# Gate modulation beside the output projection read through other buffers, and the last tile's residual and final products in another order

## The chip, the cores and the metric

The kernel runs on one core of a Trainium2 chip. The core has five engines that run side by side, each with its own queue of instructions in a fixed order: TensorE (PE in the profile: matmuls, with PEld for loading their weights), VectorE (DVE), ScalarE (ACT), GpSimd (POOL) and SyncE (SP), which here does nothing but issue transfers. They work on an on-chip memory, SBUF, and TensorE writes its results to a second one, PSUM, in banks. An engine waits for another through semaphores.

The metric is the device time of one execution in microseconds, as the median of several runs. The profile is one execution on the chip, recorded by the hardware; its span is a little shorter than the execution's device time.

## The reference

One inference step of a two-layer diffusion backbone, for 512 latent tokens and 128 context tokens (640 in all, width 1024). Each layer has a mixer (attention) and a SwiGLU feed-forward part; both are framed by an adaptive modulation whose shift, scale and gate come from a condition vector, one for the latent and one for the context tokens.

```python
for l in range(DEPTH):                       # 2 layers
    sh1, sc1, g1, sh2, sc2, g2 = split(silu(cond) @ w_mod[l] + b_mod[l], 6)
    h = rms_norm(x, norm_mix[l]) * (1 + sc1) + sh1
    x = x + g1 * mixer(h)                    # layer 0: MLA and neighbourhood attention, layer 1: GQA
    h = rms_norm(x, norm_ffn[l]) * (1 + sc2) + sh2
    gate, up = split(h @ w_ffn_in[l], 2)
    x = x + g2 * ((silu(gate) * up) @ w_ffn_out[l])
y = rms_norm(x, norm_final)
```

The part that matters here: `g2` of layer 1 (the product of 1024 numbers `silu(cond)` with 1024 columns of `w_mod[1]`, for two conditions) is computed while the output projection inside `mixer` of layer 1 runs; and the last addition to `x` and the last `rms_norm` end the kernel.

## The kernel before

The activations lie transposed: 8 tiles `x[0]` to `x[7]` of 128 features by 640 tokens. Work on tokens goes by halves of 320 (`HALF`; half 0 is called c = 0, half 1 c = 1). Each matmul of single precision is done as three faster ones, with both operands split into a high and a low part; so each weight tile is loaded as it is ("raw"), copied to its high part by ScalarE, and the low part is the difference, taken by VectorE (`lo="v"`) or GpSimd (`lo="g"`). That is `unit` (L172 to L182).

Buffers come from pools with a fixed number of slots for each tag. A read into a slot waits until everything that used the tile before it in that slot is done. Three pools matter: `rawp` with 3 slots for raw weights, `wp` with 3 for split ones, and `fp` (`op[5]`), the pool of the feed-forward part of layer 1, which is opened before the output projection (`ffn_open`, L1057) and lies where the attention's tiles lay.

The order on each engine's queue isn't the order in which the program is written. A planner goes through the program with its own estimates of durations: whenever an engine is free, it gives it the earliest written instruction whose inputs and slot are ready at that moment. The result is a fixed order for each queue, DMA issues on SP's among them. `after(inst, fn)` forbids the planner to put what `fn` writes ahead of `inst` on the same engine; it adds no wait at run time.

**The output projection of layer 1** is `mixer_out` (L980), with tiles named `oc`. It makes 8 output tiles n from 8 attention tiles. For n = 0 and 1 all but the last of the eight steps are done for both halves before the last attention tile is there; tiles 2 to 4 are done for both halves one after the other; for tiles 5 to 7 the second half is held back, and done in pieces between the modulations of the next part. `evac(n, c, ps)` adds a finished half to `x[n]` with its gate (`residual`, L316, two VectorE instructions for the second half), squares it on ScalarE and adds the square to a running sum on VectorE (`Norm.add`, L202). When half 0 of all tiles is summed, `rstd` (L212) sums over the features with a matmul by ones (tile `ocnp`), and two activations make the scale that the modulation of the feed-forward part waits for. A pair of PSUM banks is held by a tile from its first matmul to its eviction; there are four banks for tiles 0 to 6.

After each n, `beside(n)` is called: in layer 1 it is `gates_beside` (L1870), which computes the 8 x 2 gate products. For n = 0 to 3 it issues the reads of two raw tiles `wmG` of `w_mod`; for n = 1 to 4 it multiplies those of the step before with the two condition rows `cb`, 16 products of 128 x 1024 in all (`junkG`, with the sum in an accumulator that is read by a second short instruction). At n = 4 the bias is added. In layer 0 `beside` does nothing.

**The end of the kernel** is the last pass (p = 3) of the loop over pairs of output tiles at the end of `ffn` (L1547 on), which makes tiles 6 and 7 with a scheme of seven products for 2 x 2 blocks. Its steps are S2, A11, S3, A12, A22, S1 and S4. A12 gives half 0 of tile 6, A22 half 0 of tile 7, S1 (bank `c`) gives half 1 of tile 7 (with `u3`), and S4 (bank `d`) half 1 of tile 6, as the bank plus `p6`. `final` (L1887) does the last norm: a product of each tile's half with its weight and the scale, and the write of the result, on the queue of SP or of ScalarE by turns. Half 0's scale and first four products are written right after A22, the other four after S1; half 1's eight come at the very end.

Of the kernel before, what the change touches and what calls it, by code (L numbers as in the profile page):

```python
# [11 lines left out]
F32 = mybir.dt.float32  # L12
F32R = mybir.dt.float32r
AF = mybir.ActivationFunctionType
ALU = mybir.AluOpType
# [34 lines left out]
def body(ctx, tc, xT, vecs, crow, wm0, wm0g, wm1, wA, wNV, wNA, wMK, wMV, wOA, wGQ, wGK, wGV, wOC,  # L50
# [143 lines left out]


    class Norm:
        def __init__(self, name, n):
            self.name, self.n, self.k = name, n, [0, 0]
            self.acc = tmp(name + "acc")
            self.rs = tmp(name + "rs")  # L200

        def add(self, x, i):  # L202
            c0, c1 = HALF[i]
            if self.k[i] == 0:
                S.activation(self.acc[:, c0:c1], x[:, c0:c1], AF.Square)
            else:
                sq = tp.tile([P, HT], F32, tag="u", bufs=7, name=f"{self.name}sq{self.k[i]}{i}")
                S.activation(sq, x[:, c0:c1], AF.Square)
                V.tensor_add(self.acc[:, c0:c1], self.acc[:, c0:c1], sq)
            self.k[i] += 1  # L210

        def rstd(self, i):  # L212
# [767 lines left out]
    def mixer_out(wsrc, os_, order, xin, ml, name, nxt, pre, beside=lambda n: None):  # L980

        nrm = Norm(name + "n", D)
        oh, ol = [o[0] for o in os_], [o[1] for o in os_]
        x = []
        ks = [(k, k) for k in order]
        if True:
            def wunit(n):
                get = lazy(lambda: unit(wsrc[n], 1024, f"{name}w{n}", lo="g" if n % 2 else "v"))
                return lambda w0: (get(), w0)

            def evac(n, c, ps):
                if c == 0:
                    x.append(xin(n))
                residual(x[n], x[n], ps, ml, G1, n, c)
                nrm.add(x[n], c)

            def half(ps, un, c, ks, first=True, last=True):
                two_halves([ps], [un], ks, oh, ol, c, first=first, last=last)

            held = []  # L1000
            for n in range(KT):
                un = wunit(n)
                if n < 2:
                    ps = pair(f"{name}{n}")
                    for c in range(2):
                        half(ps, un, c, ks[:-1], last=False)
                    held.append((ps, un))
                    if n == 1:
                        for i, (ps, un) in enumerate(held):
                            for c in range(2):  # L1010
                                half(ps, un, c, ks[-1:], first=False)
                                evac(i, c, ps[c])
                        held = []
                elif n < 5:
                    ps = pair(f"{name}{n}")
                    for c in range(2):
                        half(ps, un, c, ks)
                        evac(n, c, ps[c])
                else:
                    ps = pair(f"{name}{n}") if n < 7 else [bank(f"{name}{n}{c}") for c in range(2)]  # L1020
                    half(ps, un, 0, ks)
                    evac(n, 0, ps[0])
                    held.append((n, ps, un))
                beside(n)
            pre()
            for j in range(KT - 2):
                for n, ps, un in held:
                    half(ps, un, 1, ks[j:j + 1], first=j == 0, last=False)
# [44 lines left out]
    def ffn(l, x, pend, hm, nxt, side, opened):  # L1073
# [418 lines left out]
        if paired:  # L1492
# [54 lines left out]
            for p in range(4):  # L1547
                n = 2 * p
                b = {c: bank(f"fo{l}_1_{p}{c}", "my"[p % 2]) for c in "abcd"}
                o = {c: tp.tile([P, HT], F32, tag="u", bufs=7, name=f"fo{l}_1_{p}{c}") for c in ("p1", "p6", "u3", "x")}  # L1550
                for k, (c, which, to) in enumerate(PLAN):
                    j = p * len(PLAN) + k
                    weights(j + LEAD)
                    seventh(j, b[to], which, c in ("S2", "A11", "S1", "S4"))
                    ps = b[to][:, :HT]
                    if c == "S2":
                        S.activation(o["p6"], ps, AF.Copy)
                    elif c == "A11":
                        S.activation(o["p1"], ps, AF.Copy)
                        V.tensor_tensor(o["p6"], o["p6"], o["p1"], ALU.add)  # L1560
                    elif c == "S3":
                        V.tensor_tensor(o["u3"], ps, o["p1"], ALU.add)
                    elif c == "A12":
                        evac(n, 0, b["a"])
                    elif c == "A22":
                        V.tensor_tensor(o["p1"], ps, o["p1"], ALU.add)
                        evac(n + 1, 0, o["p1"])
                        if p == 3:
                            nxt(x, nrm, 0, range(4))
                    elif c == "S1":  # L1570
                        V.tensor_tensor(o["u3"], ps, o["u3"], ALU.add)
                        V.tensor_tensor(o["p6"], ps, o["p6"], ALU.add)
                        evac(n + 1, 1, o["u3"])
                        if p == 3:
                            nxt(x, nrm, 0, range(4, KT))
                    else:
                        V.tensor_tensor(o["x"], ps, o["p6"], ALU.add)
                        evac(n, 1, o["x"])
# [291 lines left out]
    def gates_beside(n):  # L1870
        if n == 0:
            for c in range(2):
                S.activation(cb[c], cb[c], AF.Silu)
        while gates:
            i, raw = gates.pop(0)
            for c in range(2):
                junk = op[1].tile([P, D], mybir.dt.bfloat16, tag="junk", bufs=1, name=f"junkG{i}{c}")
                V.scalar_tensor_tensor(junk, raw, 1.0, cb[c], ALU.mult, ALU.mult, accum_out=mods[1][:, G2 + i, c:c + 1])
        if n < 4:
            gates.extend((i, load(wm1[G2 + i], D, f"wmG{i}")) for i in (2 * n, 2 * n + 1))  # L1880
        elif n == 4:
            m = mods[1][:, G2:G2 + 8, :]
            V.tensor_tensor(m, m, bc2(bmod(1, G2, 8)), ALU.add)
# [2 lines left out]

    def final(x, nrm, c, ks):  # L1887
        c0, c1 = HALF[c]
        if 0 in ks:
            nrm.rstd(c)  # L1890
        for k in ks:
            V.scalar_tensor_tensor(x[k][:, c0:c1], x[k][:, c0:c1], vcol(V_NFIN + k), nrm.rs[:, c0:c1], ALU.mult, ALU.mult)
            (nc.sync if k % 2 else nc.scalar).dma_start(yT[:, k, c0:c1], x[k][:, c0:c1])

    x, pend = ffn(1, x, pend, box["m"], final, lambda fk: lambda *a: None, op)
    pend()
# [156 lines left out]
```

## Time and profile before

| what | us |
| --- | --- |
| median of 3 runs (1527.66 to 1532.81) | 1528.15 |
| the profiled execution's own time | 1527.25 |
| its span in the profile | 1525.5 |
| TensorE busy in the span | 1461.0 |
| VectorE busy | 1191.0 |
| ScalarE busy | 768.8 |
| GpSimd busy | 223.3 |
| output projection of layer 1, first eviction to the last sum of half 0 | 1030.70 to 1076.80 |
| gate products, first and last start | 1025.3 to 1055.9 |
| last matmul of the feed-forward part to the end of the span | 1510.96 to 1525.5 |

How to read the lines that follow: in the timelines each line has the start, the length, the engine, the line of the program, the instruction, the tile written `<-` the tiles read, sizes, a count, and in brackets how long the engine stood idle before it and what ended that. In the chain of waits, a line has start, length, engine, tile and line. `SPq` is SyncE's queue of DMA issues. Busy times of engines that nobody waits for cost nothing.

### The profile page before, as it was taken

What the parts mean: (1) busy time and instruction counts of PE and PEld (TensorE: products, weight loads), DVE (VectorE), ACT (ScalarE), POOL (GpSimd) and SP (SyncE); (2) the same over time, 40 slices, a digit from 0 to 9 for tenths busy, and PEclk for the clock granted to TensorE, in tenths of its full rate; (3) what the DMA queues carried; (4) which work ended last, traced back from release to release, by engine and by line L of the source; (5) the groups of instructions that cost most, each with busy time, mean ns of one, the idle gap of its engine ahead of it and who ended that gap; (6) DMA issues with size and microseconds to landing.
All of it is one profiled execution on the core that took longest, in us unless ns stands there. A gap on an engine that the chain in (4) does not pass through costs nothing.

```text
span 1525.5 us, 25797 instructions
## 1 busy us (share of the span) xinstructions
PE 1461.0 (96%) x9856; PEld 1404.0 (92%) x9856; DVE 1191.0 (78%) x2233; ACT 768.8 (50%) x1506; POOL 223.3 (15%) x295
## 2 busy tenths in 40 slices
PE   5999989989999999999999999998999999999996
PEld 4888878879999999999999899987999999999996
DVE  5646687885899999968998777768798889854496
ACT  5445577763755455531224566662755555542242
POOL 0225634522000000000003333211100000000000
PEclk9999999999999999999999999998999999999998
DMA  9324540005155555479762300016244445458521
GB/s 370 115 95 167 174 142 30 27 23 189 38 187 174 192 190 183 163 248 344 237 217 95 103 29 29 28 33 203 70 136 162 161 163 196 157 208 303 209 91 69
DMA packets 79579, 226.89 MB, mean 149 GB/s; under 512 B 8816, under 2 KB 14208, under 8 KB 79328
## 3 DMA queue, kind: packets, MB, share of 16 engines
q1 hardware_dynamic: 77120, 220.84, 42.3%
q10 hardware_dynamic: 1920, 3.47, 0.7%
q8 instruction: 77, 1.26, 0.3%
q0 software_dynamic: 416, 0.93, 0.2%
q14 instruction: 46, 0.38, 0.1%
HBM read 190.86 MB, written 34.36 MB: 148 GB/s over the span
## 4 chain that ended last, share of the span: by engine, by line
PE 81%; DVE 10%; ACT 4%; DMA 2%; issue 2%; POOL 0%; DVEq 0%; SPq 0%; ACTq 0%; POOLq 0%
PE fg L62 19%; PE fd L62 9%; PE fo L62 7%; PE fu L62 5%; PE gq L62 2%; PE nk L62 2%; PE nq L62 2%; PE fo_2b L62 1%; PE fo_0b L62 1%; PE fo_0a L62 1%; PE fo_2a L62 1%; PE mod L62 1%; PE go L62 1%; PE gs L62 1%; PE ms L62 1%
## 5 line engine op out<-in xcount | busy, mean ns | idle before, releaser
L1098 ACT ACTIVATE sg<-g 128x320 f32<-128x320 f32 x40 | 18.9, 472 | 132.1 <-DVE g L1098 132.1
L1626 DVE SCALAR_TENSOR_TENSOR junk<-wm,cb 128x1024 bf16<-128x1024 f32 x62 | 75.6, 1220 | 6.1 <-DMA wm<-in_wm 5.5
L62 PE MATMUL gq<-h10h,wgq 128*128 128x320 f32 x256 | 66.4, 318 | 0.4 <-DVE gb L1809 0.3
L249 POOL TENSOR_SCALAR h10h<-h10t,gs,mods 128x320 fp32r<-128x320 f32 x4 | 3.6, 888 | 429.5 <-DVE h10t L243 427.8
L1098 DVE TENSOR_TENSOR wY<-s,wY 128x1024 fp32r<-128x1024 f32 x40 | 48.7, 1218 | 1.1 <-ACT wY L1098 1.1
L1098 DVE TENSOR_TENSOR wZ<-s,wZ 128x1024 fp32r<-128x1024 f32 x40 | 48.7, 1218 | 0.0
L62 PEld LDWEIGHTS gq<-h10h,wgq 128*128 128x128 f32 x256 | 45.3, 190 | 1.8 <-PE gtp L66 1.1
L1098 ACT ACTIVATE wZ<-s 128x1024 fp32r<-128x1024 f32 x40 | 42.4, 1061 | 2.3 <-DVE s L1098 2.2
L1098 ACT ACTIVATE wY<-s 128x1024 fp32r<-128x1024 f32 x40 | 42.0, 1049 | 0.0
L1098 DVE SCALAR_TENSOR_TENSOR junk<-wm,cb 128x1024 bf16<-128x1024 f32 x34 | 41.5, 1220 | 0.6
L1810 ACT ACTIVATE gp<-gs,gb,rq 128x640 f32<-128x640 f32 (+1 forms) x40 | 31.9, 797 | 19.0 <-DVE gb L1809 14.9
L1098 DVE TENSOR_TENSOR sg<-up,sg 128x640 f32<-128x640 f32 (+1 forms) x40 | 31.4, 785 | 12.2 <-ACT sg L1098 12.2
L62 PE MATMUL gq<-h10l,wgq 128*128 128x320 f32 x128 | 39.8, 311 | 0.0
L62 PE MATMUL fg<-h11q,wX 128*128 128x320 f32 x240 | 38.7, 309 | 0.9 <-DVE wX L181 0.9
L62 PE MATMUL fd<-h11D,wY 128*128 128x320 f32 x240 | 38.8, 309 | 0.5 <-DVE wY L1098 0.5
L62 PE MATMUL fg<-h11E,wW 128*128 128x320 f32 x240 | 38.7, 310 | 0.3 <-DVE g L1098 0.3
L62 PE MATMUL fu<-h11q,wX 128*128 128x320 f32 x240 | 38.7, 309 | 0.0
L62 PE MATMUL fg<-h11N,wZ 128*128 128x320 f32 x240 | 38.6, 309 | 0.0
L62 PE MATMUL fg<-h01q,wX 128*128 128x320 f32 x240 | 38.6, 309 | 0.0
L62 PE MATMUL fg<-h01N,wZ 128*128 128x320 f32 x240 | 38.6, 309 | 0.0
L62 PE MATMUL fu<-h01q,wX 128*128 128x320 f32 x240 | 38.6, 309 | 0.0
L62 PE MATMUL fg<-h01E,wW 128*128 128x320 f32 x240 | 38.6, 309 | 0.0
(3188 smaller groups left out, 5291.2 us busy)
## 6 DMA issues: line engine op xcount, KB each, us to landing
wm<-in_wm SPq DMA_DIRECT2D x40, 512.0 KB, 3.9
mraw<-in_wm SPq DMA_DIRECT2D x24, 512.0 KB, 3.6
mraw<-in_wm SPq DMA_DIRECT2D x8, 1024.0 KB, 15.3
hr_T<-sp_T SPq DMA_DIRECT2D x24, 320.0 KB, 5.9
hr_B<-sp_B SPq DMA_DIRECT2D x18, 320.0 KB, 6.9
wm<-in_wm0g SPq DMA_DIRECT2D x8, 512.0 KB, 3.4
wmG<-in_wm SPq DMA_DIRECT2D x8, 512.0 KB, 3.5
x<-in_xT SPq DMA_DIRECT2D x8, 320.0 KB, 5.6
```

The source lines that it names most:

```text
L62: cls.last = nc.tensor.matmul(*a, **k)
L249: G.tensor_scalar(h[:, c0:c1], t, self.gsl[:, k, 0:1], self.ml[:, self.sh + k, 0:1], ALU.mult, ALU.add)
L1098: self.last = after(self.last, lambda: op(*a, **k))
L1626: def step(kind, at, line=lambda op, *a, **k: op(*a, **k)):
L1810: S.activation(dst, src, AF.Exp, bias=nb, scale=rq[:, j:j + 1], accum_out=ll[:, j:j + 1])
```

## The change

The gate reads no longer take slots of `rawp`, but the two slots of tag `wr` in the feed-forward pool. The weight units of all eight tiles are made ahead as objects, and the unit of tile n + 1 (its read and its split) is written before the gate products of step n, for n = 1 to 6. The gate products are put behind the last sum of squares that is written by then (`nrm.last`), on VectorE.

At the end, half 0's scale is written after A22 without products. After S1, half 1 of tile 6 gets `p6` added at once by a residual of its own; then tile 7 is evicted, and one final product of half 0 is put behind its sum. After S4 the bank `d` is added to tile 6 by a second residual, without the addition that made `x` of it and `p6`; that eviction is put behind the one final product, and the other seven products of half 0 behind its sum.

```diff
     class Norm:
+        last = None
...
-                V.tensor_add(self.acc[:, c0:c1], self.acc[:, c0:c1], sq)
+                self.last = V.tensor_add(self.acc[:, c0:c1], self.acc[:, c0:c1], sq)
...
+            units = [wunit(n) for n in range(KT)]
             for n in range(KT):
-                un = wunit(n)
+                un = units[n]
...
-                beside(n)
+                if beside is not None:
+                    if 0 < n < KT - 1:
+                        units[n + 1](0)
+                    beside(n, nrm.last)
...
                         evac(n + 1, 0, o["p1"])
                         if p == 3:
-                            nxt(x, nrm, 0, range(4))
+                            nrm.rstd(0)
                     elif c == "S1":
                         V.tensor_tensor(o["u3"], ps, o["u3"], ALU.add)
                         V.tensor_tensor(o["p6"], ps, o["p6"], ALU.add)
-                        evac(n + 1, 1, o["u3"])
                         if p == 3:
-                            nxt(x, nrm, 0, range(4, KT))
+                            residual(x[n], x[n], o["p6"], mods[l], G2, n, 1)
+                            evac(n + 1, 1, o["u3"])
+                            ended = after(nrm.last, lambda: nxt(x, nrm, 0, range(0, 1)))
+                        else:
+                            evac(n + 1, 1, o["u3"])
+                    elif p == 3:
+                        after(ended, lambda: evac(n, 1, b["d"]))
+                        after(nrm.last, lambda: nxt(x, nrm, 0, range(1, KT)))
                     else:
                         V.tensor_tensor(o["x"], ps, o["p6"], ALU.add)
                         evac(n, 1, o["x"])
...
-                V.scalar_tensor_tensor(junk, raw, 1.0, cb[c], ALU.mult, ALU.mult, accum_out=mods[1][:, G2 + i, c:c + 1])
+                after(done, lambda: V.scalar_tensor_tensor(junk, raw, 1.0, cb[c], ALU.mult, ALU.mult,
+                                                           accum_out=mods[1][:, G2 + i, c:c + 1]))
         if n < 4:
-            gates.extend((i, load(wm1[G2 + i], D, f"wmG{i}")) for i in (2 * n, 2 * n + 1))
+            for i in (2 * n, 2 * n + 1):
+                raw = op[5].tile([P, D], F32, tag="wr", bufs=2, name=f"wmG{i}")
+                nc.sync.dma_start(raw, wm1[G2 + i])
+                gates.append((i, raw))
...
     def final(x, nrm, c, ks):
         c0, c1 = HALF[c]
-        if 0 in ks:
+        if 0 in ks and c == 1:
             nrm.rstd(c)
         for k in ks:
-            V.scalar_tensor_tensor(x[k][:, c0:c1], x[k][:, c0:c1], vcol(V_NFIN + k), nrm.rs[:, c0:c1], ALU.mult, ALU.mult)
+            last = V.scalar_tensor_tensor(x[k][:, c0:c1], x[k][:, c0:c1], vcol(V_NFIN + k), nrm.rs[:, c0:c1], ALU.mult, ALU.mult)
             (nc.sync if k % 2 else nc.scalar).dma_start(yT[:, k, c0:c1], x[k][:, c0:c1])
+        return last
```

More of the change, by code (lines that the diff above doesn't have):

```diff
@@ L978, in two_halves, with mixer_out @@
                 proj(pss[u][c], wh[0], wh[1], hh, hl, [k], *HALF[c], first=first and j == 0, last=last and j == n - 1, w0=wl)
-    def mixer_out(wsrc, os_, order, xin, ml, name, nxt, pre, beside=lambda n: None):
+    def mixer_out(wsrc, os_, order, xin, ml, name, nxt, pre, beside=None):
         nrm = Norm(name + "n", D)
@@ L1868, in body, with gates_beside @@
     gates = []
-    def gates_beside(n):
+    def gates_beside(n, done):
         if n == 0:
```

## The prediction

> **What bounds the kernel now.** First the page's head:
>
> ```profile
> span 1525.5 us, 25797 instructions
> PE 1461.0 (96%) x9856; PEld 1404.0 (92%) x9856; DVE 1191.0 (78%) x2233; ACT 768.8 (50%) x1506; POOL 223.3 (15%) x295
> ```
>
> TensorE is busy nearly throughout, so a change pays only where TensorE waits. Next, TensorE in order of time over the layer-1 output projection (tiles oc0 to oc7), where the gate modulation runs beside it, and the windows view of several stretches (columns: length, busy time of PE, PEld, DVE, ACT, POOL, granted clock, DMA share, GB/s):
>
> ```profile
> 1031.68 0.31 PE L62 MATMUL oc1b<-oGs7h,ocw 128*128 128x320 f32 x1
> 1039.04 0.63 PE L62 MATMUL oc2a<-oGs0h,ocw 128*128 128x320 f32 x1 [7.04 <-ACT ocw L180]
> ```
> ```profile
> 1025.30:1030.70 5.40, 5.40 (x39) 5.40 (x38) 3.69 (x6) 1.06 (x1) 0.00 (x0) 1.00 0.31 93
> 1030.70:1076.80 46.10, 38.51 (x239) 37.85 (x238) 37.81 (x61) 15.74 (x23) 9.95 (x4) 0.89 0.61 203
> 350.70:385.40 34.70, 34.70 (x239) 34.70 (x238) 22.91 (x33) 13.62 (x21) 9.85 (x4) 1.00 0.45 153
> 1041.00:1047.10 6.10, 6.08 (x23) 6.09 (x24) 4.83 (x8) 1.06 (x1) 0.26 (x1) 0.52 0.80 251
> 842.40:845.00 2.60, 2.60 (x6) 1.81 (x7) 0.10 (x1) 1.33 (x4) 0.99 (x2) 0.50 0.16 61
> 1520.00:1522.00 2.00, 0.00 (x0) 0.00 (x0) 2.00 (x6) 0.00 (x0) 0.00 (x0) 0.50 0.94 330
> ```
>
> After oc1 TensorE stops for 7.0 us, and when oc2 runs, from 1041 to 1047, it has a clock of 0.52: 23 matmuls in 6.1 us, 0.27 each, where the row 350.70:385.40 has 239 in 34.7, 0.145 each. Why is weight tile ocw2 late? The transfer queue and VectorE in order of time:
>
> ```profile
> 907.33 0.33 SPq L163 DMA_DIRECT2D ocw0r<-in_wOC  x1
> 926.00 19.27 SPq L163 DMA_DIRECT2D wmG<-in_wm  x2
> 963.20 0.33 SPq L163 DMA_DIRECT2D ocw1r<-in_wOC  x1
> 981.69 46.54 SPq L163 DMA_DIRECT2D wmG<-in_wm  x2
> 1034.50 0.33 SPq L163 DMA_DIRECT2D ocw2r<-in_wOC  x1
> ```
> ```profile
> 1033.25 1.22 DVE L1878 SCALAR_TENSOR_TENSOR junkG<-wmG,cb 128x1024 bf16<-128x1024 f32 x1
> ...
> 1039.74 1.22 DVE L181 TENSOR_TENSOR ocw<-ocw2r,ocw 128x1024 fp32r<-128x1024 f32 x1
> ...
> 1047.17 0.55 DVE L320 SCALAR_TENSOR_TENSOR xr<-oc2a,mods,xr 128x320 f32<-128x320 f32 x1 [1.23 <-PE oc2a L62]
> 1048.03 2.30 DVE L1878 SCALAR_TENSOR_TENSOR junkG<-wmG,cb 128x1024 bf16<-128x1024 f32 x1 [0.30 <-DMA wmG<-in_wm]
> ...
> 1057.20 2.40 DVE L1883 TENSOR_TENSOR mods<-mods,vec 128x16 f32<-128x16 f32 x1
> ...
> 1068.55 1.49 DVE L209 TENSOR_TENSOR ocnacc<-ocnacc,ocnsq 128x320 f32<-128x320 f32 x1 [0.54 <-ACT ocnsq L208]
> ```
>
> Gate reads and weights share three raw buffers. The read of ocw2 goes out at 1034.50, when the gate product that began at 1033.25 has freed one; then come its transfer, its split, and a queue of products before the low half at 1039.74.
>
> **The mixer stage, step by step.** Removed: four gate reads ahead of ocw2 in the raw buffers. At the moments at which those buffers came free (907, 926, 945, 963, 982) the new order can read ocw0 to ocw4; ocw2 then needs only a third split buffer, left by the last query tile. TensorE can go from oc1 at 1031.8 straight into oc2. The same function in layer 0, with no gates, shows that pace: from the first eviction to the last sum of squares of the first token half it takes 34.70 us (row 350.70:385.40, TensorE busy throughout), here 46.10 (row 1030.70:1076.80). TensorE alone would gain 11.4 us.
>
> But VectorE has to keep up, and here I chose against that number. In those 46.10 us VectorE is busy for 37.81. After the change it no longer splits ocw2 there (the row of 1039.74: -1.2), but the three products that now run before the first eviction (the 3.69 of row 1025.30:1030.70) must come behind it, since each waits for the last sum of squares. So 37.8 - 1.2 + 3.7 = 40.3 us of VectorE work in a stretch that TensorE could do in 34.7. **VectorE becomes the bound of this stage.**
>
> What else costs time? A sum waits half a microsecond for its square (0.54 in the row of 1068.55); with products at hand most of these waits are filled, though not the first ones: I take 1.2 us idle, from 0. And GpSimd's four weight splits hold VectorE:
>
> ```profile
> 1046.84 2.41 POOL L181 TENSOR_TENSOR ocw<-ocw3r,ocw 128x1024 fp32r<-128x1024 f32 x1 [35.25 <-ACT ocw L180]
> 1057.16 2.42 POOL L181 TENSOR_TENSOR ocw<-ocw5r,ocw 128x1024 fp32r<-128x1024 f32 x1 [7.91 <-DVE junkG L1878]
> 1067.19 2.50 POOL L181 TENSOR_TENSOR ocw<-ocw7r,ocw 128x1024 fp32r<-128x1024 f32 x1 [7.62 <-ACT ocw L180]
> ```
>
> The product of 1048.03, the addition of 1057.20 and the sum of 1068.55 each end just after such a pass. The product is 1.08 over the 1.22 of its kind, the addition of 16 columns at most 2.3 over, the sum 1.0 if without the pass it takes a third of its time: 4.4 us of GpSimd's 9.95. The eviction of 1047.17, which reads PSUM, isn't held. In a fuller VectorE more of the 9.95 is met: I take 1.0 more, from -4.4 (never met) to +5.6 (all met). The sum: 40.3 + 1.2 + 1.0 = 42.5 against 46.1, a gain of **3.6 us** (from -1.0 to 10.2, where TensorE's pace is nearly reached).
>
> The Trainium skill, page "SBUF — State Buffer", section "SBUF: two separate sides", speaks against the change here: it calls the port pair that VectorE and GpSimd share an exclusive lock, which whoever starts first holds for the whole instruction while the other "fully blocks". By that rule a VectorE without gaps meets all 9.95 us and the stage gains nothing; the trace agrees on instructions with two SBUF inputs, but only some of the passes are met.
>
> TensorE now runs ahead and waits for the ones product that follows the last sum: it could be there 11.4 us sooner, and VectorE lets it be 3.6. Held second halves fill a part of that. Elsewhere, and at the kernel's end, a waiting TensorE looks like this:
>
> ```profile
> 842.36 2.50 PE L62 MATMUL gkp<-ksq,ones 128*128 128x320 f32 x4 [2.93 <-ACT ksq L1706]
> ```
> ```profile
> 1516.14 1.45 PE fn1p L62 x2
> ```
>
> After 2.93 us of waiting it has clock 0.50 (row 842.40:845.00), and the last ones product, just as cold, takes 1.45; at the full clock I estimate about half of that and its fixed part, 0.8: **+0.6** (0 to 0.9).
>
> Covered at no cost: the gate reads on SP's queue, which can start only when the attention's tiles beneath their new buffers are free. That is some moment between 926, when the first of them went out, and the products themselves, first due at 1033; they land in 3.5 us:
>
> ```profile
> wmG<-in_wm SPq DMA_DIRECT2D x8, 512.0 KB, 3.5
> ```
>
> A weight read queued behind them on SP has the whole time since 907 to pass ahead. With two buffers a read waits for the product two tiles back: the other tile's two products, and evictions and sums between, cover it. The feed-forward weights wgu_10 and wgu_11 wait for the condition rows' buffers, which the last products free; their splits are ordered behind the modulation that follows the ones product, which covers them. GpSimd's splits of ocw3, 5 and 7 move earlier, and GpSimd has nothing else queued in the stage. The early split of ocw2 falls into the attention's tail: free in one of VectorE's waits there, 1.2 if it goes ahead of the attention's own chain: **+0.2** (0 to 1.2).
>
> **The tail, step by step.** TensorE's last block and VectorE in order of time:
>
> ```profile
> 1508.16 2.80 PE L62 MATMUL fo_3d<-hr_B,wo_3S 128*128 128x320 f32 x18
> ```
> ```profile
> 1509.17 1.93 DVE L1892 SCALAR_TENSOR_TENSOR xr<-xr,vec,fn1rs 128x320 f32<-128x320 f32 x4
> 1511.02 0.67 DVE L320 SCALAR_TENSOR_TENSOR xr<-fo_3u,mods,xr 128x192 f32<-128x192 f32 x2
> 1511.61 1.00 DVE L1892 SCALAR_TENSOR_TENSOR xr<-xr,vec,fn1rs 128x320 f32<-128x320 f32 x2
> ...
> 1513.86 0.48 DVE L1577 TENSOR_TENSOR fo_3x<-fo_3d,fo_3p 128x320 f32<-128x320 f32 x1
> 1514.38 0.68 DVE L320 SCALAR_TENSOR_TENSOR xr<-fo_3x,mods,xr 128x192 f32<-128x192 f32 x2
> 1515.59 0.49 DVE L209 TENSOR_TENSOR fn1acc<-fn1acc,fn1sq 128x320 f32<-128x320 f32 x1 [0.54 <-ACT fn1sq L208]
> 1518.67 3.79 DVE L1892 SCALAR_TENSOR_TENSOR xr<-xr,vec,fn1rs 128x320 f32<-128x320 f32 x8 [2.59 <-ACT fn1rs L217]
> ```
>
> fo_3d ends at 1510.96, but VectorE takes it at 1513.86, behind eight final products of the first half. After: from 1509.2 a residual with fo_3p (added: 0.59, as 1511.02 to 1511.61), the eviction of tile 7 (0.59), square and sum (0.54 + 0.49), one final product (0.46, a quarter of 1.85), to 1511.9; then fo_3d straight from PSUM (0.68; fo_3x is gone), square and sum, to 1513.6. The scale follows 2.59 later at the latest, at 1516.2, or 1515.5 with a warm ones product, while VectorE does the seven other products until 1516.85; eight more at 0.464 end at 1520.55, against 1518.67 + 3.79 = 1522.46: **-1.9**. Their 15 writes of 160 KB then follow each other without the pause they have now: 2.46 MB at the 330 GB/s of row 1520.00:1522.00 take 7.4 us from 1513.6, ending 0.45 later than VectorE. So from -1.4 to -2.0. The work that hides the seven products is the scale's chain; without it they cost 3.25.
>
> **Sum:** -3.6 + 0.6 + 0.2 - 1.9 = -4.7 on the profiled execution's 1527.25 us (span 1525.5 and 1.75 around it): 1522.55. The median of the runs, 1528.15, lies 0.9 above that execution, so I forecast **1523.4** for the median.
>
> **Rivals** (times as medians). (a) TensorE's pace holds: GpSimd's passes fall beside evictions, and late products behind the last sum. For it speaks layer 0; against it 40.3 us of work in 34.7. -11.4 - 1.9 gives 1514.9; chance 0.14. (b) GpSimd's passes are all met, since VectorE has no gaps: +1.0 + 0.6 + 0.2 - 1.9 = -0.1, so 1528.0; for it speak the three rows that end with a pass, against it that its waits for squares and every eviction can lie beside them; 0.13. The Trainium skill's page "SBUF — State Buffer" would have it so. (c) TensorE, cold before the ones product, also does the held second halves (72 matmuls, 10.4 us) at half clock for some 3 to 6 us, and all evictions of tiles 5 to 7 come later: half of the stage's gain is lost, 1525.2; for it the clock of 0.52 over 6.1 us after the wait of 7.04, against it that in layer 0 these halves end before VectorE wants them; 0.08. The Trainium skill's page "TensorE: Matmul & The Clock Gate", section "What's actually happening", names an idle window of about 3.4 us for this drop, and the trace shows it after 2.93. (d) The change doesn't do what it says: the planner, which orders by its own estimates, still sends ocw2's read late, and only the tail gains: 1526.3; against it the buffers free since 926; 0.10. (e) Slower: the low half of ocw4, and then of ocw6, stands in VectorE's queue behind four products, the first time with a read that is late (3.5). Each time TensorE stops for the products and a GpSimd pass (4.9 + 2.4) and goes cold (23 x 0.12 = 2.8): 2 x 10.1 + 3.5 = 23.7 against the 11.4 + 1.9 to be had, so +10.4: 1538.5. It decides from 3.9 us a stop, where 2 x (3.9 + 2.8) is 13.4; for it, those splits come behind the products in trace order; against it, any gap of VectorE lets the planner put them in early; 0.05.
>
> **Chances and range.** The forecast has 0.50, spread over about 1519 to 1526. About 0.5%, 7.6 us, is what a measurement here can tell from no change: 1520.5 and 1535.8. Faster than that: (a) and a third of the forecast's spread, 0.30; slower: (e), 0.05; within: 0.65. The range, 1516.5 to 1528.5, leaves out most of (a) and (e).
>
> **What would show it.** Right: ocw2r is read before 1000, no TensorE gap at 1032, VectorE busy for over 39 of the 42 to 43 us from the first eviction to the last sum, a TensorE wait for that sum, fo_3d read within 1.6 us of its end, 15 final products in one run. Wrong: a wait on a weight split between oc2 and oc7, or a stage of less than 38 us or more than 46.

## The result, and the profile after

The changed kernel takes 1522.75 us (median of 6 runs, 1521.07 to 1523.54), the kernel before 1529.6 beside it: a ratio of **0.9954** (95% interval 0.9941 to 0.9967), 0.46% faster. Measured once more, beside the first experiments, it was 0.9963 (0.9951 to 0.9975). The profiled execution took 1523.39 us against 1527.25, with a span of 1521.6 against 1525.5.

The transfer queue shows the first step of the change. All weights up to ocw5 are read in the attention's time, and the first gate rows only behind them:

```profile
947.28 0.33 SPq L163 DMA_DIRECT2D ocw2r<-in_wOC  x1
965.51 0.33 SPq L163 DMA_DIRECT2D ocw3r<-in_wOC  x1
984.01 0.33 SPq L163 DMA_DIRECT2D ocw4r<-in_wOC  x1
1009.62 0.33 SPq L163 DMA_DIRECT2D ocw5r<-in_wOC  x1
1019.36 0.80 SPq L1895 DMA_DIRECT2D wmG<-in_wm  x2
```

In the windows view the stage from the first eviction (1033.56) to the end of the last sum of half 0 (1076.55) takes 42.99 us, 46.10 before. VectorE is busy for 41.90 of them, and TensorE, now without the gap ahead of oc2, is done early:

```profile
1033.56:1076.55 42.99, 36.75 (x249) 36.22 (x247) 41.90 (x66) 14.64 (x22) 10.64 (x4) 0.96 0.53 174
```

TensorE in order of time, at the end of the stage and at the end of the kernel:

```profile
1076.61 1.44 PE L62 MATMUL ocnp<-ocnacc,ones 128*128 128x320 f32 x2 [5.96 <-DVE ocnacc L211]
1077.38 0.94 PE L62 MATMUL oc<-oGs2h,ocw 128*128 128x320 f32 x1
1078.11 0.47 PE L62 MATMUL oc<-oGs2l,ocw 128*128 128x320 f32 x1
...
1080.32 0.30 PE L62 MATMUL oc<-oGs3l,ocw 128*128 128x320 f32 x1
```
```profile
1506.29 2.79 PE L62 MATMUL fo_3d<-hr_B,wo_3S 128*128 128x320 f32 x18
1511.71 0.81 PE L62 MATMUL fn1p<-fn1acc,ones 128*128 128x320 f32 x2 [2.63 <-DVE fn1acc L211]
```

It waits 5.96 us for the last sum; then the ones product and some of the held halves run at a granted clock of 0.53 (the column behind GpSimd's; a matmul takes 0.47, and 0.30 afterwards):

```profile
1076.61:1080.32 3.71, 3.71 (x12) 3.32 (x13) 0.00 (x0) 2.40 (x4) 0.00 (x0) 0.53 0.72 255
```

VectorE in the stage, its long instructions with some normal ones for comparison, and GpSimd's four passes:

```profile
1036.17 1.74 DVE L211 TENSOR_TENSOR ocnacc<-ocnacc,ocnsq 128x320 f32<-128x320 f32 x1 [0.43 <-ACT ocnsq L210]
...
1042.53 1.21 DVE L1890 SCALAR_TENSOR_TENSOR junkG<-wmG,cb 128x1024 bf16<-128x1024 f32 x1
...
1043.67 0.41 DVE L322 SCALAR_TENSOR_TENSOR xr<-oc2b,mods,xr 128x192 f32<-128x192 f32 x1
1044.00 3.10 DVE L1890 SCALAR_TENSOR_TENSOR junkG<-wmG,cb 128x1024 bf16<-128x1024 f32 x1
...
1058.63 2.68 DVE L211 TENSOR_TENSOR ocnacc<-ocnacc,ocnsq 128x320 f32<-128x320 f32 x1
1061.24 3.43 DVE L1890 SCALAR_TENSOR_TENSOR junkG<-wmG,cb 128x1024 bf16<-128x1024 f32 x1
...
1074.85 0.16 DVE L1899 TENSOR_TENSOR mods<-mods,vec 128x16 f32<-128x16 f32 x1
...
1076.07 0.48 DVE L211 TENSOR_TENSOR ocnacc<-ocnacc,ocnsq 128x320 f32<-128x320 f32 x1
```
```profile
1035.15 2.42 POOL L181 TENSOR_TENSOR ocw<-ocw3r,ocw 128x1024 fp32r<-128x1024 f32 x1 [20.70 <-ACT ocw L180]
1043.06 2.96 POOL L181 TENSOR_TENSOR ocw<-ocw5r,ocw 128x1024 fp32r<-128x1024 f32 x1 [5.49 <-ACT ocw L180]
1058.32 2.65 POOL L181 TENSOR_TENSOR wgu<-wgu_1r,wgu 128x1024 fp32r<-128x1024 f32 x1 [12.30 <-ACT wgu L180]
1060.92 2.66 POOL L181 TENSOR_TENSOR ocw<-ocw7r,ocw 128x1024 fp32r<-128x1024 f32 x1
```

Each pass has one long VectorE instruction that starts inside it and ends after it: 1.74 + 3.10 + 2.68 + 3.43 for two sums of 0.48 and two products of 1.22, so 7.55 us over. The eviction of 1043.67, which starts inside the pass of ocw5 and reads PSUM, is not held. The addition to `mods`, 2.40 before, takes 0.16.

The tail on VectorE: fo_3d ends at 1509.08 and is read at 1509.96, and fifteen final products end at 1518.60, 12.31 us after fo_3d began; before it was 14.30 (1508.16 to 1522.46):

```profile
1509.96 0.67 DVE L322 SCALAR_TENSOR_TENSOR xr<-fo_3d,mods,xr 128x192 f32<-128x192 f32 x2
1511.17 0.49 DVE L211 TENSOR_TENSOR fn1acc<-fn1acc,fn1sq 128x320 f32<-128x320 f32 x1 [0.54 <-ACT fn1sq L210]
1511.58 7.02 DVE L1908 SCALAR_TENSOR_TENSOR xr<-xr,vec,fn1rs 128x320 f32<-128x320 f32 x15
```

**Where the 3.9 us between the two profiles went.** Stage lengths alone mislead here: the stage is 3.1 us shorter, yet its last sum ends at nearly the same moment in both (1076.55 and 1076.78). So I follow one engine through: for the n-th matmul of each tile, how much later does it end in one trace than in the other? The median over a window is TensorE's *offset* there, and where it changes, time was won or lost. The table gives these changes against the first profile of before, for the six profiles that bear on it (the tail is the time from fo_3d's start to the last final product).

| TensorE's offset, us | before, again | tail only | mixer only | after | after, again |
| --- | --- | --- | --- | --- | --- |
| at 600 to 800 us, ahead of all that the change touches | -0.4 | +1.9 | +1.7 | +1.5 | -0.5 |
| change to 1026 (attention) | 0.0 | 0.0 | +1.5 | +1.3 | +0.6 |
| change 1026 to 1084 (mixer stage) | -0.4 | -0.6 | -3.0 | -2.9 | -2.0 |
| change to 1290 (feed-forward, first part) | -1.4 | -1.4 | -2.6 | -2.6 | -3.1 |
| change to 1505 (feed-forward, rest) | +0.3 | +1.2 | +1.2 | +0.8 | +0.9 |
| tail (14.30 before) | 14.30 | 12.31 | 14.30 | 12.31 | 12.31 |

For the first pair: +1.5 + 1.3 - 2.9 - 2.6 + 0.8 - 2.0 = -3.9. The first of these, and 0.7 of the second, are in code that is the same in both.

### The profile page after: what moved, and what is told of

Its sections match the earlier page's. It is cut to its first block, busy times and chain, and to the rows that moved or that the text cites. A ratio compares the mean times of both kernels' runs of the same rounds, so it can differ in the third digit from the quotient of the medians.

```text
span 1521.6 us, 25799 instructions
## 1 busy us (share of the span) xinstructions
PE 1459.4 (96%) x9856; PEld 1404.0 (92%) x9856; DVE 1192.5 (78%) x2234; ACT 767.3 (50%) x1506; POOL 223.5 (15%) x295
## 4 chain that ended last, share of the span: by engine, by line
PE 77%; DVE 13%; ACT 4%; DMA 4%; issue 2%; POOL 0%; DVEq 0%; SPq 0%; ACTq 0%; POOLq 0%
PE fg L62 19%; PE fd L62 9%; PE fo L62 7%; PE fu L62 5%; PE gq L62 2%; PE nk L62 2%; PE fo_2b L62 1%; PE nq L62 1%; PE go L62 1%; DVE junkG L1890 1%; DMA mraw<-in_wm 1%; PE fo_2a L62 1%; PE ms L62 1%; PE gs L62 1%; PE mod L62 1%
## 5 line engine op out<-in xcount | busy, mean ns | idle before, releaser
L62 PE MATMUL fd<-h11q,wZ 128*128 128x320 f32 x240 | 38.6, 310 | 0.2 <-ACT p L1104 0.2
```

What stands on the lines that cost most here:

```text
L62: cls.last = nc.tensor.matmul(*a, **k)
```

## The experiments

**The same kernels again.** Both kernels, unaltered, for second profiles and closer intervals.

> The kernel before, unaltered, for a second profile and for the spread of a ratio. If the 1.5 us by which the two traces differ at 860 us and the 0.8 at 888 us, both in code that the change leaves alone and both where TensorE's clock drops, are chance from one execution to the next, this profile shows such shifts against the first one of the same kernel, of 0.5 to 2 us. If they belong to the kernel, it lies within 0.2 us of the first up to 1000 us. Ratio 1.000 in both.

> The changed kernel, unaltered, for a second profile and a closer interval. Ratio 0.9955 (0.994 to 0.997). If the shifts ahead of 1000 us are chance, this profile's TensorE stands elsewhere than +2.3 against the kernel before at 1000 us, anywhere from 0 to +2.5; if they belong to the changed kernel, it is at +2.3 again. In both the mixer stage takes 43 us and the tail 12.3.

The kernel before against itself: 0.9999 (0.9988 to 1.0010). The changed kernel: 0.9963 (0.9951 to 0.9975). The table's first row shows that shifts in untouched code are chance: over the fourteen profiles of this study the offset at 600 to 800 us lies between -1.3 and +3.0, with no order by kernel (the changed kernel's two are +1.5 and -0.5). Up to 997 us all fourteen run the same instructions in the same order on TensorE, VectorE, ScalarE and GpSimd. In the first place where such a shift arises, the clock differs. The same matmuls of 24 to 28.5 us, by the windows view, in the first profile of before and of after:

```profile
24.00:28.50 4.50, 4.50 (x33) 3.69 (x26) 3.75 (x11) 3.56 (x7) 0.00 (x0) 0.75 1.03 409
```
```profile
24.00:28.50 4.50, 4.50 (x24) 3.90 (x16) 3.29 (x8) 3.47 (x6) 0.00 (x0) 0.50 1.03 410
```

At a granted clock of 0.50 TensorE does 24 matmuls in a time in which it does 33 at 0.75. Even the last ones product of the same changed kernel, after the same wait (2.63 and 2.64), took 0.81 in one profile and 1.43 in the other, whose row is:

```profile
1509.43 1.43 PE L62 MATMUL fn1p<-fn1acc,ones 128*128 128x320 f32 x2 [2.64 <-DVE fn1acc L211]
```

The Trainium skill, page "TensorE: Matmul & The Clock Gate", section "What's actually happening", says that the activity window is free-running and doesn't start with the kernel; that would give just such differences between executions, and these rows agree with it. No run here shows the window itself.

**Each part alone.** The mixer of before with the new tail, and the new mixer with the tail of before; each leaves the other part's lines of the diff as they were.

> The mixer and the gate modulation as before, with the reordered tail alone. My theory (the tail is worth what its own rows show: from the start of fo_3d to the last final product 14.30 us before and 12.31 after, and nothing else of the change acts on it): 2.0 us less than the kernel before, ratio 0.9987, and the mixer stage unchanged at 46.1 us from the first eviction to the last sum of squares. Rival (the products of the first token half, now behind the second half's, delay the scale or the writes once the mixer isn't changed too): no gain, ratio 1.000, and the end of the span more than 3.1 us behind the last final product.

> The changed mixer stage with the tail as before. My theory (from the offsets of TensorE's matmuls between the two traces: +0.55 in the attention's end where ocw2's low half is split, -2.9 in the mixer stage, -2.4 in the first 15 us of the feed-forward stage, where the low half of wX_3 is now 7 us earlier, +0.5 later): 4.3 us less than before, ratio 0.9972. With the tail's 2.0 that is 6.3, near the 6.9 between the medians. Rival 1 (the feed-forward part of the gain was chance): 1.9 us less, ratio 0.9988, wX_3's low half again as late as 1099. Rival 2 (the stage gains nothing once its loss ahead is counted): ratio 1.000.

The tail alone: 1525.72 us, ratio 0.9985 (0.9973 to 0.9997), and from fo_3d to the end 12.31 us. The mixer alone: 1523.84, ratio 0.9976 (0.9966 to 0.9987), stage 42.93. Together 0.15% and 0.24%, about 6.0 us; the whole change was measured at 0.46% and 0.37%. Both parts are real, they add within what these intervals can tell, and the feed-forward gain belongs to the mixer part. Its place is in the rows of TensorE and VectorE where the feed-forward part begins, in the kernel before:

```profile
1091.49 0.81 PE L62 MATMUL ocnp<-ocnacc,ones 128*128 128x320 f32 x2 [1.27 <-DVE ocnacc L209]
...
1100.51 1.73 PE L62 MATMUL fg<-h11q,wX 128*128 128x320 f32 x10 [0.92 <-DVE wX L181]
```
```profile
1099.24 1.21 DVE L181 TENSOR_TENSOR wX<-wX_3r,wX 128x1024 fp32r<-128x1024 f32 x1
```

In all three profiles with the old mixer these waits are 1.25 to 1.27 and 0.92 to 0.93. In the changed kernel the low half of wX_3 is made seven microseconds sooner and its wait is gone; the one before the ones product is 0.24:

```profile
1092.21 1.22 DVE L181 TENSOR_TENSOR wX<-wX_3r,wX 128x1024 fp32r<-128x1024 f32 x1
```

That is 1.03 + 0.92 = 1.95 us, and the table's means give the same: -0.9 with the old mixer (the first profile of before counted as 0), -2.8 with the new. The means hang on few profiles, though: with the old mixer the three are 0, -1.4 and -1.4.

Why the low half of wX_3 comes sooner stays open. That its raw buffer came free sooner is not the reason. In the run with half of the products, further down, the gate reads are out of the raw buffers too, and the read of wX_3 goes out 10.7 us ahead of the ones product of half 0 (7.8 in the kernel before), but its low half begins 21.9 us behind that product, as in the kernel before (21.8), and both waits are back:

```profile
1081.22 0.81 PE L62 MATMUL ocnp<-ocnacc,ones 128*128 128x320 f32 x2 [1.27 <-DVE ocnacc L211]
...
1090.25 1.73 PE L62 MATMUL fg<-h11q,wX 128*128 128x320 f32 x10 [0.92 <-DVE wX L181]
```

In the run with three splits on VectorE the read goes out later than before (4.7 us ahead), and yet the low half begins early, 14.95 us behind. What differs is the place that the planner gives the split in VectorE's queue. The next row of the table, +0.5 with the old mixer and +1.0 with the new, isn't settled; the tail alone has it too.

**Is VectorE the bound?** Half of the gate products are left out: the second condition's gates are made from the first one's sums.

```diff
-            for c in range(2):
+            for c in range(1):
...
+            V.tensor_tensor(m[:, :, 1], m[:, :, 0], bmod(1, G2, 8), ALU.add)
+            V.tensor_tensor(m[:, :, 0], m[:, :, 0], bmod(1, G2, 8), ALU.add)
```

> Leaves out 8 of the 16 gate products: those of the second condition row; its gates are made from the first row's sums, so the second condition's gates, and with them the output, are others. VectorE loses 8 x 1.22 = 9.8 us in the stage that took 43.0 from the first eviction to the last sum. If VectorE bounds the stage: it shrinks to TensorE's pace, 34.7 (layer 0's), or a little over, 35 to 37; TensorE's wait for the last sum (5.96 in the changed kernel) falls under 1.0; the time falls by 4 to 7 us against the changed kernel, ratio to the kernel before about 0.992. If the weights' splits on GpSimd or the gate reads in two buffers hold it: the stage stays at 40 or more and TensorE still waits over 3 us.

1515.5 us, ratio 0.9922 (0.9904 to 0.9939). The stage by the windows view, and TensorE's wait for the last sum:

```profile
1030.83:1067.05 36.22, 35.60 (x243) 35.34 (x241) 31.69 (x51) 14.11 (x22) 10.50 (x4) 1.00 0.68 218
```
```profile
1067.11 0.81 PE L62 MATMUL ocnp<-ocnacc,ones 128*128 128x320 f32 x2 [0.68 <-DVE ocnacc L211]
```

The stage falls by 6.8, not by the whole 9.8, because TensorE (35.60 of 36.22 busy) now sets it. GpSimd's passes are all still there (10.50), so they aren't the bound by themselves. Of the gate reads this run says less, since their buffers come free sooner too; against them stands that VectorE was busy for 41.90 of the 42.99 us. VectorE was the bound.

**Do GpSimd's passes hold VectorE?** The odd splits go to VectorE: three at first (the first changed line), then also the one of wgu_1 (the second).

```diff
-                get = lazy(lambda: unit(wsrc[n], 1024, f"{name}w{n}", lo="g" if n % 2 else "v"))
+                get = lazy(lambda: unit(wsrc[n], 1024, f"{name}w{n}", lo="g" if n % 2 and (name != "oc" or n < 3) else "v"))
...
-                w.append(unit(wFI[l, 0, i], 1024, f"wgu{l}_{i}", "vg"[i], pool=fp))
+                w.append(unit(wFI[l, 0, i], 1024, f"wgu{l}_{i}", "vg"[i] if l == 0 else "v", pool=fp))
```

> The low halves of ocw3, ocw5 and ocw7 are made on VectorE and not on GpSimd. In the changed kernel four VectorE instructions end with a GpSimd pass: 1.74 and 2.68 for a sum that takes 0.48 elsewhere, 3.10 and 3.43 for a product that takes 1.22: 7.5 us over. If the passes hold VectorE, these go, and 3 x 1.22 = 3.7 come in: 43.0 - 7.5 + 3.7 gives a stage of 39.2 us, no sum over 0.6 and no product over 1.3, and a time 2 to 4 less than the changed kernel's (ratio to the kernel before 0.994). If the long instructions are long for another reason (gate reads arriving, ScalarE at the same memory), they stay and the splits come on top: a stage of 46 to 47, and 2 to 3 us more than the changed kernel.

> The kernel with the three splits on VectorE, unaltered, on the chip of the kernel with four, for a closer interval of its gain: ratio to the kernel before 0.9936, 0.9926 to 0.9946; the stage 40.0 us and TensorE's offset in it -9.7 against the profile of before, within 1.0. If the first measurement was a lucky one: a ratio of 0.995 or more, no better than the kernel with the three edits together (0.9946).

> The low halves of ocw3, ocw5 and ocw7 on VectorE, and the one of wgu_1 too, the last GpSimd pass in the stage: in the kernel with the three splits alone it ran for 2.96 us and one product that met it took 2.97 for 1.22. If a pass costs VectorE what it overlaps: 1.75 goes and 1.22 comes, now partly behind the last sum; the stage takes 39 us against 40.0, no product or sum in it over 1.3, and the time is 0 to 1 us less than with the three splits, ratio to the kernel before about 0.993. If such a product is long for another reason, one of 2.5 or more is still there, and the stage takes 41 us or more.

With three: 1517.38 us, ratio 0.9936 (0.9922 to 0.9951), and again 1516.57, 0.9937 (0.9923 to 0.9950). The stage takes 40.00 us in both, and TensorE gains 9.8 us on the first profile of before between 1026 and 1290 us in both. One pass is left, and with it one long product (the row of VectorE, then that of GpSimd):

```profile
1066.39 2.97 DVE L1890 SCALAR_TENSOR_TENSOR junkG<-wmG,cb 128x1024 bf16<-128x1024 f32 x1
```
```profile
1065.33 2.96 POOL L181 TENSOR_TENSOR wgu<-wgu_1r,wgu 128x1024 fp32r<-128x1024 f32 x1 [51.45 <-ACT wgu L180]
```

With the fourth split moved it is gone as well, no sum takes over 0.5 and no product over 1.3. The stage is:

```profile
1030.26:1068.50 38.24, 38.24 (x263) 38.24 (x262) 37.65 (x70) 15.01 (x22) 0.00 (x0) 1.00 0.58 180
```

1517.24 us, ratio **0.9933** (0.9921 to 0.9946). The kernels with three and with four are the fastest here that do the whole computation. Beside each other they aren't told apart (1516.57 and 1517.24), so the last 1.8 us of the stage show in the profile alone. Four splits of 1.22 were added to the engine that bounds the stage, and the stage became 4.8 us shorter, because each pass on GpSimd had been costing that engine 1.3 to 2.2. TensorE's wait for the last sum falls from 5.96 us to 1.38 with three and to none with four, and its clock in the stage is 1.00, so the slow ones product and the slow held halves go as well. With four, TensorE is busy without a gap (38.24 of 38.24): VectorE is no longer the only limit. The Trainium skill, page "Perfetto Trace Analysis", section "Optimizing Scalar/DVE Operations", warns that handing VectorE's work to GpSimd might not help, since the two share a port; here taking it back helped.

**Does the new order of the products cost?** They are no longer put behind the last sum.

```diff
-                after(done, lambda: V.scalar_tensor_tensor(junk, raw, 1.0, cb[c], ALU.mult, ALU.mult,
-                                                           accum_out=mods[1][:, G2 + i, c:c + 1]))
+                V.scalar_tensor_tensor(junk, raw, 1.0, cb[c], ALU.mult, ALU.mult, accum_out=mods[1][:, G2 + i, c:c + 1])
```

> The gate products are no longer ordered behind the last sum of squares; the buffers, the reads and all else as in the changed kernel. VectorE is idle there for 8.79 us before the first eviction (1024.77 to 1033.56). If the order is what put 3.7 us of products into a stage that VectorE bounds: four products run before the first eviction, the stage takes 38 to 40 us instead of 43.0, and the time falls by 2 to 4 us against the changed kernel (ratio to the kernel before about 0.994). If not (the products are placed ahead of evictions and sums and only trade places, or the gate reads aren't there yet): a stage of 42.5 to 44, and the time within 1 us of the changed kernel's.

1521.09 us, ratio 0.9954 (0.9940 to 0.9968), the changed kernel 0.9963 in the other comparison: too close to tell by time. The profile is clearer. Three products run before the first eviction, the first at

```profile
1026.40 1.23 DVE L1890 SCALAR_TENSOR_TENSOR junkG<-wmG,cb 128x1024 bf16<-128x1024 f32 x1 [3.61 <-ACT cb L1885]
```

and the stage takes 40.70, a little above what I expected. A fourth product met a pass and took 2.98, and TensorE waited for the low halves of ocw4 and ocw6:

```profile
1047.90 0.41 PE L62 MATMUL oc4a<-oGs0h,ocw 128*128 128x320 f32 x1 [0.66 <-DVE ocw L181]
...
1061.22 0.41 PE L62 MATMUL oc6a<-oGs0h,ocw 128*128 128x320 f32 x1 [2.50 <-DVE ocw L181]
```

The low half of ocw6 stood behind a product that met the pass of ocw7 and took 3.43 us; after the wait the granted clock is 0.54 between 1064 and 1066 us. So the new order of the products cost the changed kernel 2.3 us of the stage, and without it TensorE's wait on a weight split comes back. The feed-forward gain is gone as well: the waits there are 1.27 and 0.92 again, 1.95 us more than in the changed kernel, nearly what the stage gained.

**The split in the attention's tail.** It is ordered behind the attention's last split.

```diff
+    split_last = []
     def rsplit(src, name):
...
-        V.tensor_tensor(l, src, f(h), ALU.subtract)
+        split_last[:] = [V.tensor_tensor(l, src, f(h), ALU.subtract)]
...
-                get = lazy(lambda: unit(wsrc[n], 1024, f"{name}w{n}", lo="g" if n % 2 else "v"))
+                get = lazy(lambda: unit(wsrc[n], 1024, f"{name}w{n}", lo="g" if n % 2 else "v", behind=split_last[0] if name == "oc" and n == 2 else None))
```

> The split of ocw2 is ordered behind the last split of the attention's outputs (its place in the kernel is then the 8.79 us in which VectorE is idle); all else as in the changed kernel. If the split in the attention's tail is what costs TensorE the 0.55 us that the three kernels with the changed mixer all show between 975 and 1011 us and the others don't: that offset falls to 0.0 and TensorE goes from oc1 into oc2 without a gap; 0.5 us less in time, ratio to the kernel before about 0.9955, too little to tell by the time alone. Rival: oc2 now waits for its low half: a gap of over 0.3 us ahead of oc2, or a first eviction that is later against the end of the attention; then the time is the same or longer.

The offset's change between 870 and 1026 is +0.1, where the new mixer without this edit has +0.5 to +0.6 (and 0.7 to 0.8 more in three profiles, all of it by 890 us, ahead of the split). The split ran in VectorE's idle time, at

```profile
1022.16 1.22 DVE L181 TENSOR_TENSOR ocw<-ocw2r,ocw 128x1024 fp32r<-128x1024 f32 x1
```

The first eviction came 9.92 us after the attention's last split instead of 9.62, and the time, 1521.69 (0.9962, 0.9948 to 0.9975), is the changed kernel's.

That the 0.5 was the price of this split isn't shown, for the offset by 1012 us rises as much without it: by 0.58 here, by 0.54 in the changed kernel. It falls back after that, where the planner has given TensorE another order (from 1010.6 us of the profile of before). What all kernels with the new mixer share is another order from 997 us on: ScalarE makes the high half of ocw2 there, and VectorE the low half of oGs5 sooner. Which of these costs the 0.5 us was not tried.

**All three at once** (three splits, free products, late ocw2).

> Three of the single edits at once: the low halves of ocw3, ocw5 and ocw7 on VectorE, the gate products not ordered behind the last sum, ocw2's split ordered behind the attention's last split. If VectorE bounds the stage and each edit takes its own work out of it: 43.0 us for the changed kernel, less 3.0 (40.0 measured with the splits on VectorE) and less 2.3 (40.7 measured with the free products) gives 37.7; TensorE's pace, 36.2 with half the products left out, is the floor. Time: 0.9936 of the splits kernel less another 2 to 3 us, ratio to the kernel before 0.9915 to 0.9925, faster than the changed kernel by 5 to 7 us. Rival: free products and splits contend for the same places ahead of the evictions, oc3 or oc4 waits for its low half (0.66 us for oc4 with the free products alone) and TensorE goes cold again: a stage of 40 or more and a ratio of 0.9935 or above.

1520.35 us, ratio 0.9946 (0.9933 to 0.9958), no better than the splits alone. The rival had the numbers right (40 or more, 0.9935 or above), but not the way: neither oc3 nor oc4 waits, and the clock stays at 1.00.

```profile
1030.81:1072.01 41.20, 39.09 (x265) 38.56 (x263) 36.62 (x63) 14.06 (x22) 2.41 (x1) 1.00 0.54 180
```

VectorE's work did fall, to 36.62, but it has 4.6 us of idle time in a stage of 41.20, and TensorE waits again. The low half of ocw6 came late, behind the products, so that TensorE did held halves first and oc6 after them; and then a sum met the one pass that is left:

```profile
1061.28 0.41 PE L62 MATMUL oc6a<-oGs0h,ocw 128*128 128x320 f32 x1 [0.45 <-DVE ocw L181]
...
1072.07 0.81 PE L62 MATMUL ocnp<-ocnacc,ones 128*128 128x320 f32 x2 [1.72 <-DVE ocnacc L211]
```
```profile
1066.87 2.46 DVE L211 TENSOR_TENSOR ocnacc<-ocnacc,ocnsq 128x320 f32<-128x320 f32 x1 [1.51 <-ACT ocnsq L210]
```

**Were the shared buffers the cause?** The gate reads go back to the raw buffers; the rest of the change stays.

```diff
-                raw = op[5].tile([P, D], F32, tag="wr", bufs=2, name=f"wmG{i}")
-                nc.sync.dma_start(raw, wm1[G2 + i])
-                gates.append((i, raw))
+                gates.append((i, load(wm1[G2 + i], D, f"wmG{i}")))
```

> The changed kernel with the gate reads back in the three raw buffers that the weights use; the weights are still asked for one tile ahead, and the products are still ordered behind the last sum. If the shared buffers are what made TensorE wait (my reading): now that the products run only after the first evictions, the read of ocw3, which needs the buffer of a gate row, goes out no earlier than the product that frees it, 5 us or more after the first eviction; TensorE waits for oc3 by 3 us or more, and the stage takes 45 to 48 us against 43.0; time 1 to 4 us more than the changed kernel's, ratio to the kernel before 0.997 to 1.000. If asking a tile ahead and the order do it by themselves: no gap over 0.5 us, 43 us, ratio 0.996.

1536.19 us, ratio 1.0059 (1.0044 to 1.0075): slower than before, by more than I expected. The transfer queue, and TensorE:

```profile
1010.40 29.92 SPq L163 DMA_DIRECT2D wmG<-in_wm  x2
1043.15 0.33 SPq L163 DMA_DIRECT2D ocw3r<-in_wOC  x1
```
```profile
1047.75 0.63 PE L62 MATMUL oc3a<-oGs0h,ocw 128*128 128x320 f32 x1 [5.08 <-ACT ocw L180]
...
1050.67 0.63 PE L62 MATMUL oc3a<-oGs0h,ocw 128*128 128x320 f32 x1 [1.75 <-POOL ocw L181]
...
1070.67 0.64 PE L62 MATMUL oc5a<-oGs0h,ocw 128*128 128x320 f32 x1 [4.83 <-ACT ocw L180]
...
1073.71 0.64 PE L62 MATMUL oc5a<-oGs0h,ocw 128*128 128x320 f32 x1 [2.13 <-POOL ocw L181]
```

The wait moved from oc2 to oc3 and came a second time at oc5, and the stage takes 54.87 us, where 45 to 48 were expected. The buffers are the part of the change that removes the wait; asking a tile ahead and the order, without them, make it worse. Whether the new buffers would do without asking a tile ahead was not tried.

## Why the prediction held, step by step

**The gap at oc2 goes**: right, for the reason given (the row of ocw2r at 947.28; the run with shared buffers).

**VectorE becomes the bound at 42.5 us**: right, 42.99, and shown by the run with half the products. Inside the sum two terms were off against each other. GpSimd's hold was put at 4.4 + 1.0 = 5.4 and came to 7.55; the other VectorE work was put at 35.9 (40.3 - 4.4) and came to 34.35 (41.90 - 7.55). The second is overlap of instructions that stand back to back (the product of 1042.53 lasts 1.21, the next begins after 1.14), which a VectorE without gaps has more of: one by one, the stage's VectorE instructions add up to 41.1 us before, where it is busy for 37.8, and to 46.7 after, where it is busy for 41.9. So 3.3 and 4.8 us overlap, 1.5 more. Idle time was 1.09, put at 1.2. That the sum came within 0.5 us is in part luck: 2.15 too little for the passes, 1.55 too much for the rest.

**The cold ones product, +0.6**: 1.44 against 0.81, right. But the clock stayed low over ten of the held matmuls too. From the start of the ones product to the start of the eleventh held one it is 3.71 us (1076.61 to 1080.32), and 2.10 in the run with half the products, where TensorE waited 0.68: 1.6 in all, not 0.6. This is rival (c) at a fraction of its size. It was nearly made up for by luck: in the long wait TensorE did 24 held matmuls ahead of the ones product, 18 before, and these six (0.9 us) have no term in the sum. For TensorE the stage's gain was 2.9 in the first pair and 2.3 by the means (-0.35 with the old mixer, -2.65 with the new), where 3.6 - 0.6 = 3.0 was predicted.

**The early split of ocw2, +0.2 (0 to 1.2)**: the attention's end lost 0.5 us, within the range. The split did go ahead of work of the attention, but the late split shows that the 0.5 isn't simply its price; the cause is open.

**The tail, -1.9**: -1.99 in every profile, by the predicted order of work. A cold or a warm ones product made no difference, since VectorE does the fifteen products meanwhile.

**What I did not see**: the 1.95 us in the feed-forward part. I counted wgu_10 and wgu_11 as covered and did not ask what else of the next stage the planner would place otherwise. The step that failed is the list of what is moved: it ended with the stage, and two waits behind it (1.03 and 0.92) were missing. Why the planner moved wX_3's split stays open; the moment its raw buffer came free isn't the reason. The gain goes the same way as the rest, so the measured gain, 5.6 to 6.9 us, is larger than the 4.7 predicted; the time, 1522.75, is near 1523.4 partly because the kernel before measured 1.5 us slower beside it than in the first three runs.

**The rivals.** (a) needs VectorE to be lighter: with half of the products out, its pace is 36.2. (b) lies about as near as the forecast by its own measure, 7.55 of 10.64 us of passes met, but not by its time (1528.0). (d) is excluded by the queue. (e) did not happen here, but it does with the free products: the low halves of ocw4 and ocw6 come behind products and a pass, and TensorE stops for 0.66 and 2.50 us. With the gate reads in the raw buffers it stops twice too, 6.8 and 7.0 us each, there for late reads of ocw3 and ocw5 and then for their passes on GpSimd.

## What to carry to other kernels

When a wait is removed, add up what each engine still has to do in that stretch. The largest sum is the least that the stretch will take, and here it was a closer guide than the pace of a sister stage without that work. Count another engine's passes, where they hold the bounding engine, as work of that engine: where they cost it more than doing the job itself, take the job back. Look also at where the work of the next stage comes to stand. And before explaining a difference of 0.1% between two traces, look how far they differ in code that is the same.

## What the runs showed that I had not expected

- Identical code ahead of the change differs by up to 4.2 us (-1.3 to +3.0) between profiles, more than the tail's whole gain.
- In the changed kernel a GpSimd pass doesn't hold an instruction that already runs (the product of 1042.53, 1.21 us), nor an eviction that reads PSUM (1043.67, 0.41). What it holds ends 0.34 us after the pass where it is a sum (0.48 by itself) and 1.08 to 1.09 where it is a product (1.22), so it does nearly all of its work once the pass is over. The pass itself stretches as well, from 2.42 to as much as 2.96.
- Edits that each shortened the stage (by 3.0 and 2.3) didn't add: together they gave 41.20, longer than either alone. My reading is that the products and the splits want the same early places in VectorE's queue.
